# Layer 1's input projections by head pairs, as half tiles between the attention units

## Chip, cores and metric

The kernel runs on one core of one Trainium2 chip. The metric is the device time of one execution in microseconds (us); the number that counts is the median of the runs.

## What is computed

A two-layer transformer with two streams of 256 tokens each (latent and context, 1024 wide). Each layer has a mixer and then a hierarchical mixture of 32 experts. Layer 0's mixer is a window attention beside a latent attention; layer 1's, the one concerned here, is a differential attention with 8 heads:

```python
def _diff_mixer(h_lat, h_ctx, w_in, ..., subln, w_out, lambda_init, rope, ctx_out):
    q, k, v = _split(h @ w_in, DIFF_IN_WIDTHS)       # 1024 columns each, for both streams
    q: (b, n, 8, 2, 64)   k: (b, n, 8, 2, 64)   v: (b, n, 8, 128)
    q1_l, q2_l, k1_l, k2_l = _rope(...)              # latent stream only
    k1_all = concat([k1_l, k1_c]); k2_all, v_all likewise   # 512 keys
    a1 = _dense_attention(q1_l, k1_all, v_all, scale)
    a2 = _dense_attention(q2_l, k2_all, v_all, scale)
    o = _rmsnorm(a1 - lam * a2, subln, DIFF_EPS) * (1.0 - lambda_init)
    return o @ w_out                                 # the latent stream alone in the last layer
```

Behind it stand the residual, the norm, the router, the top two of 32 experts for 256 tokens, and a final norm.

## The kernel before

All in float32. A product that needs accuracy is made of three passes: each operand is split into a high part (float32r) and a low part, and `mm3` (line 397) multiplies high by high, high by low and low by high for each of 8 slices of the contraction. `split` (line 389) makes the high part on ScalarE (line 392), or on another engine given as `first` (line 394), and the low part by a subtraction on the engine given as `eng` (line 395).

**Loads.** Every weight comes as a tile of 128x2048 elements (1 MB) through one queue on SyncE, in the order in which `plan` lists it: the 12 tiles of layer 1's input weights (`dwin`, in the order `DWO`, with the tiles of an adaLN part between them as `ADO` says), four tiles of another adaLN part, the four tiles of the output weights (`wout1`), four more adaLN tiles, and then the experts of layer 1, six tiles each. The first four experts are fixed; the others depend on the router, and `limits` holds their loads until it has spoken. The tiles lie in a pool of 24 slots that they share with the data. `budget(n)` says that n slots are kept for data; `pump` (line 172) issues loads while the loaded tiles are below 24 less that (or less the data that stand now).

**Weight splits.** `Splits` (line 406): a `step` splits half a tile (128 columns of 256 for each of 8 slices), `get` hands out the split tile and, unless told otherwise, makes the next one at once, with the low part on VectorE.

**Layer 1's projections.** Tiles 0 to 3 of `DWO`'s numbers are queries, 4 to 7 keys, 8 to 11 values; each holds two heads. `DWO` gives the order 4, 5, 6, 8, 0, 7, 9, 1, 10, 2, 11, 3. The first key tile goes through `proj_step` into two banks `psA`; the eleven others through `k_tile`, `q_tile` and `v_tile` (lines 1665 to 1696), one after the other, each with two halves, before the first attention unit. A key half is one accumulation of 24 matmuls of 512 columns, a query half 24 of 256 (latent tokens only), a value half 48 of 256. Key and query halves get the rotary embedding in `rope_lat` (line 566: one product with the cosines in line 570, four with the sines in 573, an addition in 574, all on VectorE), then a split with the low part on GpSimd. A key half's context columns are copied by ScalarE (line 1661), a value half is copied by ScalarE (line 1694).

**Layer 1's attention.** A unit is a head and one of two query tiles of 128: 16 units. `run_units` (line 776) writes the order out by hand, and the program's order is each engine's order. In step i: scores and maximum of unit i+2; the hook of i (`early1`, line 1791); the values (`d_pv`) of unit i-1; an adaLN step, where the given function says so; the scaling (`d_scale`) of i+1; the transposes of i; the exponentials of i+2. A unit is, on TensorE, 6 score matmuls (line 1721), 4 transposes (1753) and 4 value matmuls (1765, shown as 8); on VectorE two maxima (1728), a small product (1729), a reciprocal, a small scaling (1744), the scaling and subtraction of the two maps (1746) and the output (1769); on ScalarE two exponentials (1736), a copy (1755) and a square (1768). `early1` also sets budgets, splits half tiles of the output weights on GpSimd alone (`Wo.step(GP, GP)`, at hooks 7, 9, 11 and 13) and starts the norm of the output at the end. Behind the last unit `d_turn` transposes the output, and `out_block` multiplies it with the output weights.

PSUM gives scores four banks (`psA`) and pieces, transposes and values three (`psB`).

Of the kernel before, what the change touches and what calls it, by code (L numbers as in the profile page):

```python
# [19 lines left out]
P = 128  # L20
# [32 lines left out]
DWO = (4, 5, 6, 8, 0, 7, 9, 1, 10, 2, 11, 3)  # L53
ADO = {0: (0, 1), 1: (2, 3, 4), 2: (5,), 3: (6,), 4: (7,)}
# [62 lines left out]
def model_kernel(ctx: ExitStack, tc: tile.TileContext, xin, small, cst, ada0, adaw, win, wuq, wukv, wout0, dwin,  # L117
# [24 lines left out]
    def free(n):  # L142
        st_["data"] -= n
# [422 lines left out]
    def rope_lat(ps, dst, p0, cosn, sinn):  # L566

        t = U((SEQ,))
        r = U((SEQ,))
# [1080 lines left out]
    h_lo(1, KC - 1, xb, *h13(KC - 1), True)  # L1650
    fill(2)
# [6 lines left out]

    def k_out(j, ps):
        dst = U()  # L1660
        ACT.copy(dst[:, SEQ:], ps[:, SEQ:])
        rope_lat(ps, dst, 0, "cosA", "sinA")
        split(*(x[j // 4].v[:, j % 4, :] for x in k1), dst, GP)

    def k_tile(j2):
        ws = W1.get()
        for j in range(2):
            ps = psB()
            s = slice(j * P, (j + 1) * P)
            mm3(ps, KC, lambda k: (ws[0][:, k, s], ws[1][:, k, s]), h13)  # L1670
            k_out(2 * j2 + j, ps)
        free(2)

    def q_tile(j2):
        ws = W1.get()
        for j in range(2):
            ps = psB()
            s = slice(j * P, (j + 1) * P)
            mm3(ps[:, 0:SEQ], KC, lambda k: (ws[0][:, k, s], ws[1][:, k, s]),
                lambda k: tuple(x[:, 0:SEQ] for x in h13(k)))  # L1680
            dst = U((SEQ,))
            rope_lat(ps, dst, 0, "cosA", "sinA")
            split(*(x.v[:, 2 * j2 + j, :] for x in q1), dst, GP)
        free(2)

    def v_tile(j):
        ws = W1.get()
        for t2 in range(2):
            ps = psB()
            for t in range(2):  # L1690
                ts_ = slice((2 * t2 + t) * P, (2 * t2 + t + 1) * P)
                mm3(ps[:, t * 256:(t + 1) * 256], KC, lambda k: tuple(x[:, ts_] for x in h13(k)),
                    lambda k: (ws[0][:, k, :], ws[1][:, k, :]))
            ACT.copy(v1[j // 2].v[:, 2 * t2:2 * t2 + 2, (j % 2) * 256:(j % 2 + 1) * 256],
                     ps.rearrange("p (t n) -> p t n", t=2))
        free(2)
# [11 lines left out]
    budget(18)  # L1708
    for j in DWO[1:]:
        (q_tile, k_tile, v_tile)[j // 4](j % 4)  # L1710
    free(4)
# [300 lines left out]
```

## Time and profile before

| | us |
|---|---|
| median of 3 runs | 1483.35 (1480.6 to 1484.48) |
| the profiled execution | 1484.73 |
| its span, first to last instruction | 1482.6 |
| TensorE busy | 1304.1 (88% of the span) |
| VectorE busy | 602.1 (41%) |
| ScalarE busy | 384.5 (26%) |
| GpSimd busy | 128.0 (9%) |

The profile is one execution on the chip. PE is TensorE's matmuls, PEld its weight loads, DVE VectorE, ACT ScalarE, POOL GpSimd, SPq the load queue of SyncE. A row of a timeline gives the start in us, the duration in us, engine, line, operation, output and inputs, and how many instructions it merges; in brackets stands the idle time in front of it and what ended that. Matmuls overlap in their records, so the distance from start to start is what one costs. PEclk is the granted clock of TensorE, 1.00 being 2.4 GHz.

### The profile page before, as it was taken

What the parts mean: (1) busy time and instruction counts of PE and PEld (TensorE: products, weight loads), DVE (VectorE), ACT (ScalarE), POOL (GpSimd) and SP (SyncE); (2) the same over time, 40 slices, a digit from 0 to 9 for tenths busy, and PEclk for the clock granted to TensorE, in tenths of its full rate; (3) what the DMA queues carried; (4) which work ended last, traced back from release to release, by engine and by line L of the source; (5) the groups of instructions that cost most, each with busy time, mean ns of one, the idle gap of its engine ahead of it and who ended that gap; (6) DMA issues with size and microseconds to landing.
All of it is one profiled execution on the core that took longest, in us unless ns stands there. A gap on an engine that the chain in (4) does not pass through costs nothing.

```text
span 1482.6 us, 21587 instructions
## 1 busy us (share of the span) xinstructions
PE 1304.1 (88%) x8341; PEld 724.3 (49%) x8341; DVE 602.1 (41%) x1476; ACT 384.5 (26%) x819; POOL 128.0 (9%) x110
## 2 busy tenths in 40 slices
PE   6996999989999999989878999888998787788856
PEld 4673667955445343525326897584442231323313
DVE  4488896453322322222227756944321110111102
ACT  4445655331111110101115333643110010101002
POOL 1134011220000000000013111301000000000000
PEclk9998999999999999999999999999999999998999
DMA  9634715279999999999999228357999999999995
GB/s 382 266 114 152 273 48 211 90 307 374 399 420 422 421 421 420 421 422 420 408 412 382 86 86 304 135 219 276 422 420 422 421 421 420 422 421 421 421 412 228
DMA packets 70075, 487.08 MB, mean 329 GB/s; under 512 B 7632, under 2 KB 7760, under 8 KB 13392
## 3 DMA queue, kind: packets, MB, share of 16 engines
q1 hardware_dynamic: 69968, 485.65, 80.7%
q8 instruction: 68, 1.11, 0.3%
q14 instruction: 39, 0.32, 0.1%
HBM read 484.57 MB, written 1.05 MB: 328 GB/s over the span
## 4 chain that ended last, share of the span: by engine, by line
DMA 25%; PE 16%; DVE 6%; ACT 2%; issue 1%; DVEq 0%; SPq 0%; ACTq 0%
DMA s<-in_ew_dram 25%; PE psA L1336 3%; PE psA L1368 3%; PE psB L403 2%; PE psB L404 2%; PE psB L402 2%; DVE t L1728 1%; DVE u L1746 1%; DVE s L395 1%; PE psA L402 1%; PE psA L403 1%; PE psA L404 1%; PE psB L1385 1%; DVE u L573 0%; DVE s L1378 0%
## 5 line engine op out<-in xcount | busy, mean ns | idle before, releaser
L1336 PE MATMUL psA<-s 128*32 128x512 f32 (+2 forms) x2336 | 418.3, 621 | 81.4 <-DMA s<-in_ew_dram 71.6
L1336 PEld LDWEIGHTS psA<-s 128*32 128x32 f32 (+2 forms) x2336 | 113.7, 122 | 362.7 <-issue 206.2
L1378 DVE SCALAR_TENSOR_TENSOR s<-psB,modT,s 128x256 f32<-128x256 f32 x296 | 120.4, 476 | 215.6 <-PE psB L1385 215.5
L1368 PE MATMUL psA<-s,u 128*32 128x512 f32 (+1 forms) x1168 | 185.9, 601 | 12.8 <-DMA s<-in_ew_dram 11.4
L1373 DVE SCALAR_TENSOR_TENSOR u<-psA,t,u 128x512 fp32r<-128x512 f32 x48 | 36.0, 751 | 233.0 <-ACT u L1372 233.0
L1368 PEld LDWEIGHTS psA<-s,u 128*32 128x32 f32 (+1 forms) x1168 | 53.6, 119 | 123.7 <-issue 95.4
L1510 DVE TENSOR_TENSOR u<-u,psA 128x512 f32<-128x512 f32 x24 | 16.5, 688 | 224.3 <-PE psA L1336 224.3
L1385 PE MATMUL psB<-u 128*128 128x512 f32 (+1 forms) x384 | 95.8, 369 | 13.1 <-DVE s L1378 4.6
L1362 ACT COPY u<-psB 128x512 f32<-128x512 f32 x24 | 14.1, 587 | 332.6 <-PE psB L1360 332.6
L402 PE MATMUL psB<-s 128*128 128x256 f32 (+1 forms) x296 | 96.0, 324 | 3.9 <-DVE s L895 3.9
L403 PE MATMUL psB<-s 128*128 128x256 f32 (+1 forms) x296 | 95.2, 322 | 0.4 <-DVE s L395 0.4
L404 PE MATMUL psB<-s 128*128 128x256 f32 (+1 forms) x296 | 95.1, 321 | 0.0
L1385 PEld LDWEIGHTS psB<-u 128*128 128x128 f32 x384 | 58.7, 188 | 72.1 <-issue 35.7
L1372 ACT ACTIVATE u<-psA,t 128x512 fp32r<-128x512 f32 x48 | 33.0, 688 | 177.2 <-PE psA L1368 171.6
L1507 ACT ACTIVATE u<-psA 128x512 f32<-128x512 f32 x24 | 14.4, 600 | 220.8 <-PE psA L1336 220.8
L1319 PE MATMUL psB<-s 128*128 128x256 f32 x544 | 68.0, 285 | 0.7 <-ACT u L1362 0.7
L395 DVE TENSOR_TENSOR s<-s 128x1024 fp32r<-128x1024 f32 (+3 forms) x56 | 51.6, 967 | 39.9 <-ACT s L392 39.8
L1319 PEld LDWEIGHTS psB<-s 128*128 128x128 f32 x544 | 65.9, 191 | 2.6 <-issue 1.6
L402 PEld LDWEIGHTS psB<-s 128*128 128x128 f32 x296 | 56.4, 190 | 13.8 <-DVE s L895 4.8
L402 PE MATMUL psA<-s 128*128 128x256 f32 (+1 forms) x208 | 62.6, 301 | 0.0
L403 PE MATMUL psA<-s 128*128 128x256 f32 (+1 forms) x208 | 60.5, 291 | 0.0
L404 PE MATMUL psA<-s 128*128 128x256 f32 (+1 forms) x208 | 60.4, 291 | 0.0
(349 smaller groups left out, 1736.6 us busy)
## 6 DMA issues: line engine op xcount, KB each, us to landing
s<-in_ew_dram SPq DMA_DIRECT2D x376, 1024.0 KB, 19.8
s<-in_adaw_dram SPq DMA_DIRECT2D x40, 1024.0 KB, 7.5
s<-in_dwin_dram SPq DMA_DIRECT2D x12, 1024.0 KB, 10.3
s<-in_ada_dram SPq DMA_DIRECT2D x8, 1024.0 KB, 19.8
s<-in_wout_dram SPq DMA_DIRECT2D x8, 1024.0 KB, 7.7
s<-in_ew_dram SPq DMA_DIRECT2D x16, 512.0 KB, 14.4
s<-in_win_dram SPq DMA_DIRECT2D x5, 1024.0 KB, 19.9
s<-in_xin_dram SPq DMA_DIRECT2D x2, 1024.0 KB, 8.6
```

Of the source, the lines that this page charges most:

```text
L395: eng.tensor_tensor(lo, src, hi.bitcast(F32), ALU.subtract)
L402: PE.matmul(ps, lh, rh, start=(k == 0), stop=False)
L403: PE.matmul(ps, lh, rl, start=False, stop=False)
L404: PE.matmul(ps, ll, rh, start=False, stop=(k == n - 1))
L1319: PE.matmul(ps[:, i * n:(i + 1) * n], src(t, cs_(c0 + i)), oh[:, t, 0:n], start=(t == 0 and a == 0), stop=(t == T_ - 1 and a == 1))
L1336: PE.matmul(ps[sl, :], xg(hf * 4 + k, sl), wt(m, hf)[:, k, :], start=(hf == 0 and k == 0), stop=(hf == 1 and k == 3))
L1368: PE.matmul(ps[sl, :], ht[:, k, sl], wt(2, hf)[:, k, :], start=(k == 0), stop=(k == 3))
L1372: ACT.activation(yh, ps, AF.Copy, scale=gsl)
L1373: DVE.scalar_tensor_tensor(out=yl, in0=ps, scalar=gsl, in1=yh.bitcast(F32), op0=ALU.mult, op1=ALU.subtract)
L1378: DVE.scalar_tensor_tensor(out=xc(c)[:, HALF[s]], in0=ps[:, HALF[s]], scalar=modT[:, l, 5, c, s:s + 1], in1=xc(c)[:, HALF[s]], op0=ALU.mul ...
L1385: PE.matmul(ps[:, 0:nt], ysp[a][:, cs_(q)], oht[:, 0:nt], start=(a == 0), stop=(a == 1))
L1510: TT(hm, sl, pm[1], ALU.mult)
```

## The change

The key, query and value tiles come in the order of head pairs: key 0, query 0, value 0, key 1, query 1 and so on (`DWO`), and the adaLN tiles that go with them move (`ADO`). `k_tile`, `q_tile` and `v_tile` become `k_piece`, `q_piece` and `v_piece`, which do one half each. `piece` takes the next half from a list, and behind it issues the split of half a tile of weights for the tile after it, with the low part on GpSimd (`W1.step(GP)`). The first four halves (query 0, value 0) stand ahead of the units, with the scores and exponentials of units 0 and 1 between them; the other 18 stand in the hooks of units 0 to 12, one or two each (`PIECES`). The hook runs behind the scores of unit i+2. The steps of the output weights move from hooks 7, 9, 11, 13 to 12, 13, 14, 15, the adaLN steps to hooks 2, 6, 10 and on, and the budgets change. Temporaries of the rotary embedding, the query halves and the squares move from the pool `u` to the context halves of the residual (`room`, eight in turn), which nothing reads any more.

```diff
--- before.py
+++ after.py
@@ -50,8 +50,10 @@
 
 ADL = 3
 
-DWO = (4, 5, 6, 8, 0, 7, 9, 1, 10, 2, 11, 3)
-ADO = {0: (0, 1), 1: (2, 3, 4), 2: (5,), 3: (6,), 4: (7,)}
+PIECES = {0: 1, 1: 2, 2: 1, 3: 1, 4: 2, 5: 2, 6: 1, 7: 1, 8: 2, 9: 2, 10: 1, 11: 1, 12: 1}
+
+DWO = (4, 0, 8, 5, 1, 9, 6, 2, 10, 7, 3, 11)
+ADO = {0: (0, 1), 1: (2, 3, 4), 5: (5,), 8: (6,), 11: (7,)}
 
 
 
@@ -563,10 +565,9 @@
     DVE.tensor_copy(UB, csv("U"))
 
 
-    def rope_lat(ps, dst, p0, cosn, sinn):
-
-        t = U((SEQ,))
-        r = U((SEQ,))
+    def rope_lat(ps, dst, p0, cosn, sinn, tr=None):
+
+        t, r = tr or (U((SEQ,)), U((SEQ,)))
         DVE.tensor_tensor(t[p0:P], ps[p0:P, 0:SEQ], csv(cosn)[p0:P], ALU.mult)
         for q in range(p0 // 32, 4):
             a, b = slice(32 * q, 32 * q + 32), slice(32 * (q ^ 1), 32 * (q ^ 1) + 32)
@@ -1648,6 +1649,7 @@
             W1.step()
         xb = xa
     h_lo(1, KC - 1, xb, *h13(KC - 1), True)
+    budget(19)
     fill(2)
     ps = psB()
     PE.matmul(ps[:, 0:2], onesM, lp, start=True, stop=True)
@@ -1656,44 +1658,57 @@
     DVE.tensor_scalar(nlam, lamt[:, 2:3], -LAMBDA_INIT, None, op0=ALU.add)
     k1 = [[S((4, NTOK), F32R) for _ in range(2)] for _ in range(2)]
 
+
+    rooms_ = [0]
+
+    def room():
+        rooms_[0] += 1
+        return xc(rooms_[0] % KC)[:, SEQ:]
+
     def k_out(j, ps):
         dst = U()
         ACT.copy(dst[:, SEQ:], ps[:, SEQ:])
-        rope_lat(ps, dst, 0, "cosA", "sinA")
+        rope_lat(ps, dst, 0, "cosA", "sinA", (room(), room()))
         split(*(x[j // 4].v[:, j % 4, :] for x in k1), dst, GP)
 
-    def k_tile(j2):
-        ws = W1.get()
-        for j in range(2):
-            ps = psB()
-            s = slice(j * P, (j + 1) * P)
-            mm3(ps, KC, lambda k: (ws[0][:, k, s], ws[1][:, k, s]), h13)
-            k_out(2 * j2 + j, ps)
-        free(2)
-
-    def q_tile(j2):
-        ws = W1.get()
-        for j in range(2):
-            ps = psB()
-            s = slice(j * P, (j + 1) * P)
-            mm3(ps[:, 0:SEQ], KC, lambda k: (ws[0][:, k, s], ws[1][:, k, s]),
-                lambda k: tuple(x[:, 0:SEQ] for x in h13(k)))
-            dst = U((SEQ,))
-            rope_lat(ps, dst, 0, "cosA", "sinA")
-            split(*(x.v[:, 2 * j2 + j, :] for x in q1), dst, GP)
-        free(2)
-
-    def v_tile(j):
-        ws = W1.get()
-        for t2 in range(2):
-            ps = psB()
-            for t in range(2):
-                ts_ = slice((2 * t2 + t) * P, (2 * t2 + t + 1) * P)
-                mm3(ps[:, t * 256:(t + 1) * 256], KC, lambda k: tuple(x[:, ts_] for x in h13(k)),
-                    lambda k: (ws[0][:, k, :], ws[1][:, k, :]))
-            ACT.copy(v1[j // 2].v[:, 2 * t2:2 * t2 + 2, (j % 2) * 256:(j % 2 + 1) * 256],
-                     ps.rearrange("p (t n) -> p t n", t=2))
-        free(2)
+    def k_piece(j2, j, ws):
+        ps = psB()
+        s = slice(j * P, (j + 1) * P)
+        mm3(ps, KC, lambda k: (ws[0][:, k, s], ws[1][:, k, s]), h13)
+        k_out(2 * j2 + j, ps)
+
+    def q_piece(j2, j, ws):
+        ps = psB()
+        s = slice(j * P, (j + 1) * P)
+        mm3(ps[:, 0:SEQ], KC, lambda k: (ws[0][:, k, s], ws[1][:, k, s]),
+            lambda k: tuple(x[:, 0:SEQ] for x in h13(k)))
+        dst = room()
+        rope_lat(ps, dst, 0, "cosA", "sinA", (room(), room()))
+        split(*(x.v[:, 2 * j2 + j, :] for x in q1), dst, GP)
+
+    def v_piece(j, t2, ws):
+        ps = psB()
+        for t in range(2):
+            ts_ = slice((2 * t2 + t) * P, (2 * t2 + t + 1) * P)
+            mm3(ps[:, t * 256:(t + 1) * 256], KC, lambda k: tuple(x[:, ts_] for x in h13(k)),
+                lambda k: (ws[0][:, k, :], ws[1][:, k, :]))
+        ACT.copy(v1[j // 2].v[:, 2 * t2:2 * t2 + 2, (j % 2) * 256:(j % 2 + 1) * 256],
+                 ps.rearrange("p (t n) -> p t n", t=2))
+
+
+    pieces = [(j, n) for j in DWO[1:] for n in range(2)]
+    cur = []
+
+    def piece(n=1):
+        for _ in range(n):
+            j, i = pieces.pop(0)
+            if i == 0:
+                cur.append(W1.get(False))
+            (q_piece, k_piece, v_piece)[j // 4](j % 4, i, cur[0])
+            W1.step(GP)
+            if i:
+                cur.pop()
+                free(2)
 
     wl = [W1.get(False)]
     pss = [psA() for _ in range(2)]
@@ -1705,12 +1720,7 @@
     free(2)
     q1 = [S((KC, SEQ), F32R) for _ in range(2)]
     v1 = [S((4, 512)), S((4, 512))]
-    budget(18)
-    for j in DWO[1:]:
-        (q_tile, k_tile, v_tile)[j // 4](j % 4)
-    free(4)
     oD = S((16, P))
-    budget(11)
 
     def d_scores(u):
         h, qt = u
@@ -1764,7 +1774,7 @@
         for b in range(4):
             PE.matmul(ps[:, 0:P], PT[:, b * P:(b + 1) * P], v1[h // 4].v[:, b, (h % 4) * P:(h % 4 + 1) * P],
                       start=(b == 0), stop=(b == 3))
-        sq = U((P,))
+        sq = room()[:, 0:P]
         ACT.activation(sq, ps[:, 0:P], AF.Square, scale=rec, accum_out=ssD[:, 0, 2 * h + qt:2 * h + qt + 1])
         DVE.tensor_scalar(oD.v[:, 2 * h + qt, :], ps[:, 0:P], rec, None, op0=ALU.mult)
 
@@ -1789,12 +1799,14 @@
         DVE.scalar_tensor_tensor(out=lo, in0=ps, scalar=sl1, in1=hi.bitcast(F32), op0=ALU.mult, op1=ALU.subtract)
 
     def early1(i):
-        if i in {2: 13, 10: 14}:
-            budget({2: 13, 10: 14}[i])
+        piece(PIECES.get(i, 0))
         if i == 9:
             free(3)
-            budget({2: 13, 10: 14}[10])
-        if i in (7, 9, 11, 13):
+            budget(16)
+        if i == 12:
+            free(4)
+            budget(14)
+        if i in (12, 13, 14, 15):
             Wo.step(GP, GP)
         if i == 14:
 
@@ -1808,8 +1820,12 @@
             d_norm(2)
             d_turn(1)
 
-    run_units([(h, qt) for h in range(8) for qt in range(2)], d_scores, d_max, d_exp, d_scale, d_transpose, d_pv,
-              lambda i: i in (1, 2, 3, 14, 15), early1, 3)
+    units = [(h, qt) for h in range(8) for qt in range(2)]
+    piece(2)
+    ex1 = {i: d_exp(units[i], *d_max(units[i], d_scores(units[i]))) for i in range(2)}
+    piece(2)
+    run_units(units, d_scores, d_max, d_exp, d_scale, d_transpose, d_pv,
+              lambda i: i in (2, 6, 10, 11, 12, 13, 14, 15), early1, ex=ex1)
     d_rstd(12, 16)
     d_norm(3)
     d_turn(2)
```

## Rows read from the trace of the kernel before

**Rows 1.** Busy time by stretches: length, PE, PEld, DVE, ACT, POOL, clock, DMA, GB/s.
```profile
805.20:907.60 102.40, 102.05 (x721) 96.07 (x719) 63.72 (x112) 33.00 (x51) 14.80 (x14) 1.00 0.36 126
907.60:976.70 69.10, 56.70 (x372) 38.28 (x371) 60.90 (x132) 43.77 (x122) 15.90 (x10) 0.90 0.62 241
...
1086.30:1455.60 369.30, 296.12 (x1662) 103.84 (x1662) 54.67 (x137) 33.64 (x59) 1.90 (x1) 0.95 1.01 420
```

**Rows 2.** Timeline of the load queue (SPq), 911 us to 1030 us.
```profile
911.24 99.84 SPq L170 DMA_DIRECT2D s<-in_ew_dram  x19
...
1028.25 0.80 SPq L170 DMA_DIRECT2D s<-in_ew_dram  x2
```

**Rows 3.** Timeline of PE: first matmuls of the projection halves, and the last.
```profile
805.21 0.39 PE L402 MATMUL psB<-s 128*128 128x512 f32 x1
...
826.97 0.28 PE L402 MATMUL psB<-s 128*128 128x256 f32 x1
...
907.47 0.28 PE L404 MATMUL psB<-s 128*128 128x256 f32 x1
```

**Rows 4.** Timeline of PE, one unit: scores, values, adaLN, transposes, next scores.
```profile
924.50 0.97 PE L1721 MATMUL psA<-s 64*128 64x512 f32 x6
925.39 1.16 PE L1765 MATMUL psB<-s,u 128*128 128x128 f32 x8
926.48 1.07 PE L324 MATMUL psC<-s,scS 128*32 128x512 f32 x8
927.48 0.65 PE L1753 MATMUL psB<-identR,u 128*128 128x128 f32 x4
928.07 0.97 PE L1721 MATMUL psA<-s 64*128 64x512 f32 x6
```

**Rows 5.** Timeline of DVE: the first product and the addition of one rope.
```profile
809.96 0.42 DVE L570 TENSOR_TENSOR u<-psA,u 128x256 f32<-128x256 f32 x1 [1.00 <-ACT u L1661]
...
812.15 0.43 DVE L574 TENSOR_TENSOR u<-u 128x256 f32<-128x256 f32 x1
```

**Rows 6.** Groups by shape, 805.2 to 907.6 us: xcount | busy us, mean ns.
```profile
L395 DVE TENSOR_TENSOR s<-s 128x1024 fp32r<-128x1024 f32 x22 | 27.0, 1266 | 25.8 <-ACT s L392 25.8
...
L392 ACT CAST s<-s 128x1024 fp32r<-128x1024 f32 x20 | 20.0, 1048 | 0.0
...
L392 ACT CAST s<-u 128x256 fp32r<-128x256 f32 x7 | 2.8, 406 | 24.1 <-DVE u L574 24.1
```

**Rows 7.** Timeline of POOL: low parts of key, query and weight half.
```profile
813.37 1.30 POOL L395 TENSOR_TENSOR s<-u,s 128x512 fp32r<-128x512 f32 x1 [2.35 <-ACT s L392]
...
846.38 0.74 POOL L395 TENSOR_TENSOR s<-u,s 128x256 fp32r<-128x256 f32 x1 [10.40 <-ACT s L392]
...
927.72 2.38 POOL L395 TENSOR_TENSOR s<-s 128x1024 fp32r<-128x1024 f32 x1 [2.56 <-PE psC L324]
```

**Rows 8.** Timeline of DVE: the scaling of three units.
```profile
927.92 2.72 DVE L1746 SCALAR_TENSOR_TENSOR u<-u,t 128x512 f32<-128x512 f32 x1
...
944.78 0.75 DVE L1746 SCALAR_TENSOR_TENSOR u<-u,t 128x512 f32<-128x512 f32 x1
...
947.54 0.75 DVE L1746 SCALAR_TENSOR_TENSOR u<-u,t 128x512 f32<-128x512 f32 x1
```

**Rows 9.** Timeline of PE: three waits, start of the output projection.
```profile
938.10 1.12 PE L1753 MATMUL psB<-identR,u 128*128 128x128 f32 x4 [4.77 <-DVE u L1746]
...
968.59 0.66 PE L1753 MATMUL psB<-identR,u 128*128 128x128 f32 x4 [2.26 <-DVE u L1746]
...
976.07 0.63 PE L1786 MATMUL psB<-identR,s 128*128 128x128 f32 x4 [1.47 <-DVE s L1781]
976.45 0.36 PE L402 MATMUL psA<-s 128*128 128x256 f32 x1
```

**Rows 10.** Busy time by stretches, columns as in rows 1.
```profile
935.00:940.00 5.00, 1.90 (x8) 1.48 (x10) 4.93 (x5) 1.48 (x5) 4.84 (x4) 0.56 0.31 131
940.00:945.00 5.00, 4.86 (x28) 3.44 (x27) 4.82 (x12) 3.12 (x10) 1.38 (x1) 0.76 0.50 165
```

## Prediction

> **What bounds the kernel now.** I read the busy time by stretches first, from the end of the span backwards, then the load queue, then the timelines of the stage that changes. From 1086 us to 1456 us the load of expert weights is what TensorE waits for: the DMA share is 1.01 and 420 GB/s pass, about 2.5 us for a tile of 1 MB [rows 1]. So the end of the kernel is the time at which that stream gets going, plus a fixed volume. The stream can't go ahead of the router of layer 1: only the 24 tiles of the four fixed experts may be asked for before it, and the slots of SBUF run out at 19 of them; between 1011 us and 1028 us no load is issued at all, until the first expert matmuls free slots [rows 2]. Whatever moves the end of layer 1's mixer moves that restart by the same amount.
>
> The mixer has two stages. From 805.2 us (the end of the first key tile) to 907.6 us TensorE projects: 102.0 of 102.4 us busy at clock 1.00, VectorE 63.7. From 907.6 us to 976.5 us it does the sixteen attention units, the clock is 0.90, and VectorE has 60.9 of 69.1 us [rows 1]. The change can only win what TensorE loses in the second stage, so I count its work at full clock.
>
> - Projection halves, by the starts of their first matmuls: four key halves from 805.21 to 826.97, so 5.44 us each; the matmuls of 256 columns follow at 0.12 us, so a query half (24 of them) takes 2.88 us and a value half (48) 5.76 us [rows 3]. The 22 pieces that the change moves: 6 x 5.44 + 8 x 2.88 + 8 x 5.76 = 101.7 us.
> - One unit: scores 0.89, values 1.09, transposes 0.59, from start to start; an adaLN step 1.00 [rows 4]. Sixteen units 41.1 us; seven steps and two closings (0.6 each) 8.2 us; four turns of the output at 0.6, 2.4 us.
>
> Together 153.4 us. From 805.2 us that would end at 958.6 us; the output projection really starts at 976.45 us [rows 9]. The difference, 17.9 us, is all that a perfect interleave could win.
>
> **What the change moves, and what new waits cost.** It takes no matmul away. It puts TensorE's pieces between units, so that VectorE's 2.76 us per unit (the steady distance of two scalings [rows 8]) no longer sets the pace. For that it makes TensorE depend on fresh results within a few us, which the old order never did: there the scores began with data tens of us old. I walked through the new order with the old durations.
>
> *Durations off TensorE.* A rope runs from 809.96 to 812.58, 2.62 us, and for a key half it starts behind ScalarE's copy of the other half of the bank (it sat 1.00 us idle for it) [rows 5]. The high part of a query half is a ScalarE cast of 0.41 us, that of a weight half 1.05 us. The low part of a weight half was VectorE's at 1.27 us, 22 of them, 27.0 us, all under a busy TensorE, so taking them from VectorE gains nothing by itself [rows 6]. It becomes GpSimd's at 2.38 us; a low part of a key half takes 1.30 us there, of a query half 0.74 us [rows 7]. GpSimd works in order, so the low part of a query stands behind the weight half issued before it, and the next weight half behind the query.
>
> *Opening.* Both ropes of the first key tile end at 812.58 us as now. TensorE does Q0a and Q0b from 805.2 to 811.0 us and then wants the scores of unit 0. Q0a's rope can only start at 812.6 and ends at 815.2; its high part is there at 815.65. Wait: 4.65 us. Scores of two units end at 817.7. V0a then needs all 256 columns of its weights' low part (its second matmul reads them). GpSimd does Q0a's low part to 816.4, the first half of V0's weights to 819.0, Q0b's low part, the second half to about 823.0 (822.1 if nothing is held). Wait: 5.3 us, at least 4.4. Opening 10.0 us, at least 9.1.
>
> *Each later pair of heads.* The hook of units 1, 5 and 9 issues a key half and a query half; the next scores need that query half. Behind it TensorE has the values and transposes, 1.7 us. Until the low part is there: GpSimd gets the key's low part 3.7 us after the key half ends (copy, rope, cast), has it done at 5.0, the weight half at 7.35, the query's low part at 8.1 us; the query half ended at 2.88, so 5.2 us later. Four of the six score matmuls can go with the high part, 0.6 us. Wait: 5.2 - 0.6 - 1.7 = 2.9 us; if GpSimd were free it would be 1.5 us. The second wait is the value half's. The second half of its weights is cast and subtracted behind the second query half: rope 2.6, cast 0.4, cast of the weights 1.05, GpSimd 2.38: 6.4 us after that query half. TensorE has values, an adaLN step, transposes, scores and one matmul in between, 3.7 us. Wait: 2.7 us. So 5.6 us a pair, at least 4.2.
>
> *VectorE held by GpSimd.* A scaling of 128x512 that takes 0.75 us took 2.72 us when a GpSimd subtraction ran from 927.72 to 930.10; it ended 0.5 us behind that [rows 7, 8]. It reads two operands from SBUF. So does the last step of a rope, the addition in line 574, and no row shows that one held by a long subtraction: its price lies between 0 and 2.4 us each time it meets one. In the walk it meets one in the query rope of each pair (the weight half runs from 5.0 to 7.35, the addition is due at 5.2), of which 0.7 us reach TensorE after the order of GpSimd is counted. I take 0.7, nearer to the scaling's row than to nothing: 6.3 us a pair, three pairs 18.9 us.
>
> The Trainium skill states for this (SBUF — State Buffer, section SBUF: two separate sides) that a VectorE instruction with two SBUF inputs and a GpSimd instruction that reads SBUF exclude each other for the whole instruction, whoever comes first. The trace agrees for the scaling (2.72 against 0.75 us); for the addition no run here shows it. With the rule the addition is held and a pair waits 6.3 us; without it 5.6 us, and the sum would be 2.1 us lower. The rule speaks against the change, which gives GpSimd 22 more subtractions.
>
> *Closing.* Before, TensorE sat idle 2.26 us and 1.47 us in the chain from the last scaling to the output projection [rows 9]. That chain stays: 3.7 us.
>
> *Clock.* After the idle 4.77 us that ended at 938.10 [rows 9] the granted clock was 0.56 and 0.76 in the next two stretches of 5 us [rows 10]: 3.4 us at the lower level, 1.7 us of work lost. The opening has two idles of that size, 3.4 us. The six idles of some 3 us in the pairs may cost 1.7 us each too, or nothing: 0 to 10.2 us; I take nothing, since they are shorter.
>
> *Output weights.* The four steps of Wo, a cast and a subtraction on GpSimd each, stood in the middle of the attention; they belong to that 4.77 us idle and the low clock after it, 6.5 us. Now they stand behind GpSimd's last projection work, which ends about when V3a starts. If they run under V3a and V3b they cost nothing; if their slots come free only after V3b they hold VectorE in the last three units, where no piece covers it. 0 to 6.5 us; I take 0.
>
> *Loads.* The budget holds loads to five slots until unit 9, so the output weights, the last adaLN part and the expert tiles come later. From unit 9 to the end of the mixer there are about 50 us, twenty tiles at 2.5 us, and about 18 are needed to stand where the old kernel stood; the idle from 1011 us to 1028 us covers what is late. If it does not, each tile costs 2.5 us. The temporaries that move into dead halves of the residual cost nothing: they are the same instructions on the same shapes.
>
> **The sum.** 10.0 + 18.9 + 3.7 + 3.4 = 36.0 us of waiting and low clock where there were 17.9 us: 18.1 us longer. The profiled execution took 1484.73 us (span 1482.6 and 2.1 around it), the median of the runs is 1483.35 us; I add to the median: 1501 us.
>
> **The rivals.**
> - *The waits in the pairs vanish (faster).* If the ropes, casts and subtractions of a query half reach TensorE within the 1.7 us and 3.7 us of other work, only opening and closing are left: 9.1 + 3.7 = 12.8 against 17.9 us, 5.1 us shorter, 1478 us. It decides at 1.7 us of waiting a pair. For it: VectorE and GpSimd are each busy less than TensorE in the new stage. Against it: the rope alone is 2.62 us, and GpSimd's order is fixed. Chance 0.13.
> - *The waits are near that point (no change).* One of a pair's two waits hides and the other shrinks, so 1.7 to 3 us a pair: 1480 to 1487 us. Chance 0.07.
> - *The later router is partly absorbed.* 19 of the 24 fixed tiles are issued before it [rows 2]; were five more slots free by then, 12.5 us of the stream would be gone: 1489 us. Against it: the budgets at that place are unchanged. Chance 0.10.
> - *The costs left out come in full.* Low clock in the pairs 10.2 us and Wo 6.5 us: 1518 us. For it: the gaps come every 10 to 20 us. Chance 0.15.
> - That the loads come too late for the experts would look like the last one and is held in it.
>
> My forecast has 0.55. All but the first two cases are slower by over 0.3% (4.4 us, about what a measurement of this kernel can tell from no change): slower 0.80, same 0.07, faster 0.13. The least of the forecast's own terms, 9.1 + 3 x 4.2 + 3.7 = 25.4, gives 1491 us. The range goes from 1487, below that, to 1518.
>
> **What would show it.** In the trace after: PE idle of 4 to 5 us before the first scores and before the first value half; before the scores of units 4, 8 and 12 idle of about 3 us ended by a GpSimd subtraction; before V1a, V2a and V3a idle of about 2.7 us ended by one too; the additions of the query ropes longer than 0.43 us; the output projection starting near 994 us; the expert stream as long as before. If TensorE runs through these places, the first rival is right and my walk has a latency wrong. If the output projection starts late and the end does not follow, the loads are what I misread.

## The result

| | before | changed |
|---|---|---|
| median of the runs, us | 1481.97 (1480.48 to 1484.48) | 1520.94 (1515.97 to 1521.93) |
| profiled execution, us | 1484.73 | 1521.14 |
| its span | 1482.6 | 1519.4 |
| end of the first key tile | 805.0 | 803.1 |
| first matmul of the output projection | 976.45 | 1012.34 |
| from there to the end of the span | 506.2 | 507.1 |

The ratio is 1.0254, with an interval of 1.0226 to 1.0283: 39 us slower. The forecast was 1501 us, with a range up to 1518 us. The direction was right, the size half of what came.

Busy time of the changed kernel by stretches (length, PE, PEld, DVE, ACT, POOL, granted clock, DMA share, GB/s): the whole stage from the first key tile to the output projection, what follows up to the experts, and the eight stretches inside the stage in which the clock is at its lower level.

```profile
803.05:1012.34 209.29, 170.78 (x1090) 144.98 (x1089) 123.77 (x224) 75.59 (x172) 77.70 (x44) 0.88 0.37 138
1012.34:1053.00 40.66, 36.05 (x313) 33.15 (x311) 18.96 (x41) 14.95 (x29) 9.50 (x10) 1.00 0.67 265
811.20:824.90 13.70, 7.01 (x29) 5.50 (x30) 10.90 (x21) 5.89 (x13) 7.43 (x5) 0.50 0.19 61
855.60:862.40 6.80, 5.91 (x26) 5.12 (x27) 4.50 (x8) 3.54 (x9) 3.23 (x3) 0.50 0.00 0
869.20:872.60 3.40, 2.97 (x14) 2.97 (x15) 2.51 (x5) 0.14 (x2) 0.37 (x1) 0.50 0.02 5
906.80:913.60 6.80, 5.64 (x25) 4.85 (x26) 4.83 (x8) 3.54 (x9) 3.50 (x3) 0.50 0.00 0
920.40:923.80 3.40, 2.82 (x13) 2.82 (x14) 2.66 (x5) 0.28 (x2) 0.53 (x1) 0.50 0.11 45
958.00:964.80 6.80, 5.63 (x25) 4.84 (x26) 4.84 (x8) 3.53 (x9) 3.51 (x3) 0.50 0.45 159
971.60:975.00 3.40, 2.82 (x13) 2.82 (x14) 2.66 (x5) 0.78 (x4) 0.53 (x1) 0.50 0.94 381
1002.40:1009.20 6.80, 5.77 (x26) 5.52 (x27) 3.67 (x9) 2.11 (x5) 0.00 (x0) 0.50 1.01 424
```

Before, the two halves of this stage lasted 171.5 us, with the clock at 1.00 and 0.90 [rows 1]. Now it is one stage of 209.3 us at a mean clock of 0.88. All that the kernel lost is here: the part behind it takes 0.9 us more. In the eight short stretches the clock is at its lower level, 0.50 (1.2 GHz), through and through: 51.1 us, in 38.6 of which TensorE is busy. In the kernel before there are three such stretches with 13.6 us, 11.1 of them busy. Each of the eight begins inside one of TensorE's waits; the next view shows those of the opening, of two pairs and of the closing.

Timeline of PE in the changed kernel: the longest idle times of the opening, of the first two pairs of heads and of the closing (in brackets, with what ended them), and the start of the output projection:

```profile
813.92 2.93 PE L1731 MATMUL psA<-s 64*128 64x512 f32 x12 [4.73 <-ACT s L394]
818.98 0.58 PE L404 MATMUL psB<-s 128*128 128x256 f32 x1 [2.13 <-ACT s L394]
821.40 0.58 PE L405 MATMUL psB<-s 128*128 128x256 f32 x1 [1.84 <-POOL s L397]
...
856.50 1.65 PE L1731 MATMUL psA<-s 64*128 64x512 f32 x6 [3.40 <-ACT s L394]
...
867.21 0.38 PE L404 MATMUL psB<-s 128*128 128x256 f32 x1 [0.73 <-ACT s L394]
...
869.63 0.58 PE L405 MATMUL psB<-s 128*128 128x256 f32 x1 [2.04 <-POOL s L397]
...
907.96 1.65 PE L1731 MATMUL psA<-s 64*128 64x512 f32 x6 [4.76 <-ACT s L394]
...
918.55 0.38 PE L404 MATMUL psB<-s 128*128 128x256 f32 x1 [0.73 <-ACT s L394]
...
920.98 0.58 PE L405 MATMUL psB<-s 128*128 128x256 f32 x1 [2.04 <-POOL s L397]
...
1003.43 1.09 PE L1796 MATMUL psB<-identR,s 128*128 128x128 f32 x4 [3.90 <-DVE s L1791]
...
1012.34 0.36 PE L404 MATMUL psA<-s 128*128 128x256 f32 x1
```

L1731 are scores, L404 and L405 here the first and second matmul of a value half. The third pair repeats the second (4.70, 0.73 and 2.04 us); the six other idle times are 0.5 to 1.5 us each. The sum of all idle in the stage is 38.5 us; it was 12.6 us.

How the first wait of the second pair of heads comes about, seen from VectorE (timeline of the changed kernel; the additions that close a key rope and a query rope):

```profile
902.41 0.42 DVE L575 TENSOR_TENSOR u<-s 128x256 f32<-128x256 f32 x1
...
905.07 2.40 DVE L575 TENSOR_TENSOR s<-s 128x256 f32<-128x256 f32 x1
```

and from GpSimd (key half, weight half, query half):

```profile
903.62 1.27 POOL L397 TENSOR_TENSOR s<-u,s 128x512 fp32r<-128x512 f32 x1 [5.51 <-ACT s L394]
904.85 2.34 POOL L397 TENSOR_TENSOR s<-s 128x1024 fp32r<-128x1024 f32 x1
907.99 0.73 POOL L397 TENSOR_TENSOR s<-s 128x256 fp32r<-128x256 f32 x1 [0.80 <-ACT s L394]
```

and from ScalarE (the casts of the query half and of the next weight half):

```profile
907.51 1.35 ACT L394 CAST s<-s 128x256 fp32r<-128x256 f32 x2 [3.01 <-DVE s L575]
```

The key's addition takes 0.42 us, the query's 2.40: the weight half on GpSimd holds it from 905.07 to 907.2. The cast that waits for it starts at 907.51, the scores begin at 907.96 with the high part, and the query's low part follows on GpSimd at 907.99. It is the same hold as that of the scaling before [rows 8], now on an addition.

### The profile page after: what moved, and what is told of

It is laid out like the page before. It is cut to its first block, busy times and chain, and to the rows that moved or that the text cites. A ratio compares the mean times of both kernels' runs of the same rounds, so it can differ in the third digit from the quotient of the medians.

```text
span 1519.4 us, 21585 instructions
## 1 busy us (share of the span) xinstructions
PE 1321.8 (87%) x8341; PEld 734.4 (48%) x8341; DVE 601.1 (40%) x1456; ACT 383.1 (25%) x819; POOL 175.0 (12%) x130
## 4 chain that ended last, share of the span: by engine, by line
DMA 24%; PE 17%; DVE 6%; ACT 2%; issue 1%; POOL 1%; DVEq 0%; SPq 0%; POOLq 0%; ACTq 0%
DMA s<-in_ew_dram 24%; PE psA L1337 4%; PE psA L1369 2%; PE psB L405 2%; PE psB L404 2%; PE psB L406 2%; POOL s L397 1%; DVE s L574 1%; DVE s L575 1%; ACT s L394 1%; PE psA L1731 1%; PE psB L1320 1%; PE psA L404 1%; PE psA L405 1%; PE psB L1775 1%
## 5 line engine op out<-in xcount | busy, mean ns | idle before, releaser
L1337 PE MATMUL psA<-s 128*32 128x512 f32 (+2 forms) x2336 | 425.4, 637 | 75.7 <-DMA s<-in_ew_dram 66.9
L404 PE MATMUL psB<-s 128*128 128x256 f32 (+1 forms) x296 | 102.8, 347 | 9.4 <-ACT s L394 4.3
L405 PE MATMUL psB<-s 128*128 128x256 f32 (+1 forms) x296 | 100.8, 340 | 8.0 <-POOL s L397 8.0
L397 POOL TENSOR_TENSOR s<-s 128x1024 fp32r<-128x1024 f32 (+1 forms) x40 | 82.0, 2052 | 199.6 <-ACT s L394 135.5
L1511 DVE TENSOR_TENSOR u<-u,psA 128x512 f32<-128x512 f32 x24 | 16.5, 688 | 223.0 <-PE psA L1337 223.0
L406 PE MATMUL psB<-s 128*128 128x256 f32 (+1 forms) x296 | 99.9, 337 | 0.5 <-POOL s L397 0.5
L404 PEld LDWEIGHTS psB<-s 128*128 128x128 f32 x296 | 61.5, 208 | 25.3 <-issue 8.7
L405 PEld LDWEIGHTS psB<-s 128*128 128x128 f32 x296 | 61.8, 209 | 12.5 <-POOL s L397 8.8
L1320 PEld LDWEIGHTS psB<-s 128*128 128x128 f32 x544 | 65.9, 191 | 2.6 <-issue 1.6
L394 ACT CAST s<-s 128x1024 fp32r<-128x1024 f32 (+3 forms) x71 | 53.8, 799 | 40.7 <-DVE s L575 32.2
L406 PEld LDWEIGHTS psB<-s 128*128 128x128 f32 x296 | 61.6, 208 | 5.0 <-POOL s L397 0.7
## 6 DMA issues: line engine op xcount, KB each, us to landing
s<-in_ew_dram SPq DMA_DIRECT2D x376, 1024.0 KB, 19.8
s<-in_dwin_dram SPq DMA_DIRECT2D x12, 1024.0 KB, 11.9
s<-in_ew_dram SPq DMA_DIRECT2D x16, 512.0 KB, 14.5
```

Of the source, the lines that this page charges most:

```text
L394: ACT.copy(hi, src)
L397: eng.tensor_tensor(lo, src, hi.bitcast(F32), ALU.subtract)
L404: PE.matmul(ps, lh, rh, start=(k == 0), stop=False)
L405: PE.matmul(ps, lh, rl, start=False, stop=False)
L406: PE.matmul(ps, ll, rh, start=False, stop=(k == n - 1))
L1320: PE.matmul(ps[:, i * n:(i + 1) * n], src(t, cs_(c0 + i)), oh[:, t, 0:n], start=(t == 0 and a == 0), stop=(t == T_ - 1 and a == 1))
```

## The experiments

Each starts from the changed kernel unless it says otherwise. Stage is the time from the end of the first key tile to the output projection in the profiled execution; idle is the sum of TensorE's idle in it; the rest is stage less idle less the 153.4 us of work at full clock.

| kernel | time, us | stage | idle | rest |
|---|---|---|---|---|
| before | 1482 to 1483 | 171.5 | 12.6 | 5.5 |
| changed | 1520.9 | 209.3 | 38.5 | 17.4 |
| e1_split_ahead | 1501.3 | 190.2 | 27.7 | 9.1 |
| e2_query_unit_ahead | 1521.9 | 211.0 | 41.1 | 16.5 |
| e3_four_pieces_first | 1529.2 | 217.9 | 44.7 | 19.8 |
| e4_keep_busy | 1512.6 | 202.1 | 20.8 | |
| e5_low_part_on_vector | 1519.0 | 206.8 | 38.9 | 14.5 |
| e6_ahead_vector | 1507.9 | 194.7 | 32.0 | 9.3 |
| e7_all_waits | 1495.7 | 182.9 | 22.4 | 7.1 |
| e8_all_waits_vector | 1504.8 | 192.1 | 27.5 | 11.2 |
| e9_sum_from_psum | 1500.1 | 188.2 | 25.0 | 9.8 |
| e10_waits_and_psum | 1495.9 | 183.4 | 22.6 | 7.4 |
| e11_before_wo | 1477.3 | 164.7 | 11.1 | 0.2 |
| e12_after_wo | 1520.5 | 209.2 | 38.9 | 16.9 |

The rest of e4 is left out, since it has more matmuls. Three things stand in this table before any single run is read. The stage's length carries the time of the kernel: from 6.8 us less (e11) to 46 us more (e3) than before, the time differs by as much within 3 us. And the rest grows with the idle: with 22 to 28 us of idle it is 7 to 11 us, with 38 to 45 us it is 14 to 20 us. And e11, the one run whose clock is 1.00 in the whole stage, has a rest of 0.2 us, so the 153.4 us of work hold.

**Weights split ahead of the piece.**

```diff
-            (q_piece, k_piece, v_piece)[j // 4](j % 4, i, cur[0])
             W1.step(GP)
+            (q_piece, k_piece, v_piece)[j // 4](j % 4, i, cur[0])
```

> Starts from the changed kernel (1520.9 us). One edit: the half tile of weights for the next tile is split ahead of the piece, not behind it, so that its cast and its GpSimd subtraction no longer stand behind the rope and split of the query half. Theory (the order of GpSimd and ScalarE makes TensorE wait): the waits of the value halves (2.0 + 0.7 us, three pairs, and 4.0 us in the opening) go, and the waits of the scores fall from 3.4 to 4.8 us to some 1.5 to 2.5 us, because the low part of the query half has only its rope in front of it; idle 38.5 us falls by 17 to 20 us, and some of the low clock behind the waits goes with it: 1491 to 1504 us. Rival (the rope's own time makes the waits): only the value halves gain, 8 us, 1511 to 1514 us. Rival (GpSimd's hold on VectorE makes them): as many holds as before, so no gain, 1518 to 1523 us.

1501.3 us (1.0129 of before, 1.0106 to 1.0153): 19.6 us faster than the change, the largest step of all. The waits of the value halves are gone, as the theory of the order wants. The waits of the scores are not down to 1.5 to 2.5 us, and that of the opening grew from 4.73 to 6.74 us. Timeline of PE:

```profile
849.13 1.60 PE L1731 MATMUL psA<-s 64*128 64x512 f32 x6 [4.05 <-ACT s L394]
...
894.96 1.65 PE L1731 MATMUL psA<-s 64*128 64x512 f32 x6 [4.39 <-ACT s L394]
```

and of POOL (weight half, then the query's low part):

```profile
846.02 2.34 POOL L397 TENSOR_TENSOR s<-s 128x1024 fp32r<-128x1024 f32 x1
849.15 0.73 POOL L397 TENSOR_TENSOR s<-s 128x256 fp32r<-128x256 f32 x1 [0.80 <-ACT s L394]
```

The cast of the weight half still stands behind the key half's cast on ScalarE, so its subtraction lands on the query's addition (2.41 us long, from 846.23) as before. Order is the cause of the value waits; for the score waits this run leaves order and hold together.

**The query half a unit earlier.** `PIECES` becomes 3, 1, 1, 1 for each pair in place of 1, 2, 1, 1, 2 and so on.

```diff
-PIECES = {0: 1, 1: 2, 2: 1, 3: 1, 4: 2, 5: 2, 6: 1, 7: 1, 8: 2, 9: 2, 10: 1, 11: 1, 12: 1}
+PIECES = {0: 3, 1: 1, 2: 1, 3: 1, 4: 3, 5: 1, 6: 1, 7: 1, 8: 3, 9: 1, 10: 1, 11: 1}
```

> Starts from the changed kernel. One edit: the first query half of a pair comes one unit earlier (three pieces in the hooks of units 0, 4 and 8, one in the others), so a whole piece stands between it and the scores that need it. Theory: the three waits of the scores (3.4, 4.8 and 4.7 us) go and those of the value halves (2.0 + 0.7 us a pair) stay; idle falls by 11 to 13 us and low clock by some 5 us: 1502 to 1510 us. Rival (the waits only move to the next piece, since GpSimd has the same work in the same order): 1517 to 1523 us.

1521.9 us, no gain: the theory's number was wrong and the rival's right. The scores of the pairs no longer wait; the value half does, twice as long (5.5 in place of 2.8 us). Timeline of PE:

```profile
867.52 0.58 PE L404 MATMUL psB<-s 128*128 128x256 f32 x1 [3.61 <-ACT s L394]
...
869.95 0.58 PE L405 MATMUL psB<-s 128*128 128x256 f32 x1 [1.84 <-POOL s L397]
```

Three pieces in one hook bunch the ropes and splits, and the value half behind them takes the wait over. The additions of the three query ropes that moved took 0.43, 0.51 and 0.58 us, so the hold is nearly gone here, and the idle is 41.1 us all the same. Room for one consumer is taken from another as long as the chain ahead of both has the same length.

**Four pieces before the first scores.** `piece(4)` stands ahead of `ex1`, and the second `piece(2)` goes.

> Starts from the changed kernel. One edit: all four pieces of the opening come before the scores of units 0 and 1. Theory (what TensorE waits for in the opening is the low part of the second half of the value weights, behind two query halves on GpSimd, and the scores in between are covered by that): the wait moves from the scores to the value half, which begins at the same time as now; nothing is won and the scores come behind it: 1520 to 1524 us. Rival (the place of the scores is the cause): 4.7 us and their low clock go, 1513 to 1517 us.

1529.2 us, 8 us slower, 5 us beyond the theory's interval. The wait moves to the value half, as the theory said:

```profile
820.51 0.58 PE L404 MATMUL psB<-s 128*128 128x256 f32 x1 [9.76 <-ACT s L394]
```

and behind it the scores of unit 2 wait 3.3 us for the exponentials that empty their banks, which the theory did not have.

**Matmuls in the waits.**

```diff
     def v_piece(j, t2, ws):
+        if t2 == 0:
+            idle(8)
...
+    def idle(n):
+        ps = psB()
+        for _ in range(n):
+            PE.matmul(ps, identR, h13(0)[0], start=True, stop=True)
...
     def d_scores(u):
         h, qt = u
+        if u == (0, 0):
+            idle(20)
+        if u in ((2, 0), (4, 0), (6, 0)):
+            idle(12)
```

> Starts from the changed kernel. Matmuls that nothing reads are added where TensorE waits: 20 before the scores of unit 0, 12 before those of units 4, 8 and 12, 8 before the first half of each value tile, 0.23 us each; they fit into the waits at full clock. Theory (17 us of the 55.6 us that the stage loses are the lower level of the clock, which follows the waits): the clock stays near 1.00 in the stage and 8 to 14 us come back, 1507 to 1513 us, with the waits as long as before. Rival (the clock falls for another reason than TensorE's waiting): no change, or up to 3 us slower, 1520 to 1524 us.

1512.6 us (1.0204, 1.0181 to 1.0226): with more work on TensorE the kernel is 8.3 us faster. The stage, same columns as above:

```profile
800.83:1002.95 202.12, 181.19 (x1179) 150.58 (x1177) 123.87 (x224) 75.59 (x172) 78.03 (x44) 0.97 0.39 143
```

The clock is 0.97 in place of 0.88 and the stage 7.2 us shorter. TensorE is busy at the lower level for 11.4 us in place of 38.6. So the lower level of the clock that comes with the waits is a cost of its own, of at least this size: the 88 added matmuls take some 20 us themselves (88 times 0.23), and the idle falls by 17.7 us only. They do not fill all waits (1.0 to 1.9 us stay ahead of the three groups of 12, for their bank), and one of these groups ran at the lower level itself.

**The low part on VectorE**, behind the piece (`W1.step(DVE)`) and then also ahead of it.

> Starts from the changed kernel (1520.9 us). One edit: the low part of the weight halves goes back from GpSimd to VectorE, in the same place behind the piece. Theory (order): VectorE then holds no rope addition behind GpSimd, but the subtraction stands in VectorE's own queue, between the ropes of the key and the query half, behind ScalarE's cast, so the score waits stay at 4 to 5 us; the value waits fall by 1.1 us a pair, and the opening's by about 2 us: 1513 to 1519 us. Rival (GpSimd's hold on the rope addition, 2 us each, is the greater part of the waits): 8 to 10 us of idle and their low clock go, 1502 to 1509 us.

> Both edits: weights split ahead of the piece and their low part on VectorE. The first alone gave 1501.3 us; its three score waits are 4.1 to 4.4 us and in each the addition of the query rope is held 2.0 us by GpSimd's weight half. Theory (order): the weight half's subtraction takes the same place in VectorE's queue, since ScalarE casts it behind the key half; the score waits stay: 1498 to 1505 us. Rival (hold): three times 2 us and some low clock go, 1490 to 1496 us.

1519.0 and 1507.9 us. Taking all weight halves off GpSimd, and with them every hold on a rope (all additions take 0.42 or 0.43 us), gains nothing that the intervals show (1.0198 to 1.0269 of before, against 1.0226 to 1.0283), and where they are split ahead it is 6.5 us slower by the medians (1.0146 to 1.0202 against 1.0106 to 1.0153). Timeline of PE in the first of the two:

```profile
907.42 1.65 PE L1731 MATMUL psA<-s 64*128 64x512 f32 x6 [5.24 <-ACT s L394]
...
919.50 0.38 PE L405 MATMUL psB<-s 128*128 128x256 f32 x1 [0.88 <-DVE s L397]
```

The score wait is 5.2 us and so longer than with the hold (4.76), the second part of the value wait 0.9 in place of 2.0 us. VectorE works in order too, and its subtraction now stands between the two ropes. So the rival's gain does not come by this way; but the hold is exchanged here for 1.3 us of work on VectorE, and what the hold alone is worth is seen in e9. e6 came out slower than the theory had it.

**All waits at once.** Split ahead; value tile 0 ahead of query tile 0 in `DWO`; `piece(5)` ahead of the first scores and no `piece(2)` behind them; `PIECES` 2, 1, 1, 1 and then 3, 1, 1, 1 twice. The second with `W1.step(DVE)`.

> Everything that the waits rest on is moved: weights split ahead of the piece, the first query half of a pair one unit earlier, the first value tile ahead of the first query tile, and the scores of units 0 and 1 behind the first key half of pair 1. GpSimd keeps the low parts. Theory (what the change loses is its waits and the low clock behind them): idle falls from 38.5 us to the closing's 7 us and 2 to 4 us more, the low clock from 17 us to 3 to 6 us; the stage then loses 12 to 17 us against 17.9 us in the kernel before: 1475 to 1483 us. Rival (holds between GpSimd and VectorE and the three PSUM banks make new waits as the old ones go): 1488 to 1500 us.

> As e7_all_waits, with the low part of the weight halves on VectorE. Theory (order; with room in front of every consumer it doesn't matter which engine subtracts): within 4 us of e7_all_waits. Rival (hold): 5 us or more faster than it.

1495.7 us (1.0096, 1.0067 to 1.0125) and 1504.8 us. The idle falls by 16 us and the rest by 10 us, but not as far as expected, and the kernel stays slower than before; the rival's range holds. Timeline of PE in the first:

```profile
834.97 2.31 PE L1731 MATMUL psA<-s 64*128 64x512 f32 x6 [4.41 <-ACT u L1746]
...
900.16 0.36 PE L404 MATMUL psB<-s 128*128 128x256 f32 x1 [1.94 <-DVE s L574]
```

The scores of unit 2 wait for the exponentials that empty their banks (4.41 us), and the first value half of a pair waits 1.4 to 1.9 us until the rope has read the bank of the query half ahead of it. Those are the rival's new waits, on PSUM banks. On VectorE it is 9 us worse, which neither theory had.

**The addition without the hold**, on top of e1.

```diff
-        DVE.tensor_tensor(t[p0:P], ps[p0:P, 0:SEQ], csv(cosn)[p0:P], ALU.mult)
+        if tr:
+            t = ps[:, 0:SEQ]
+        else:
+            DVE.tensor_tensor(t[p0:P], ps[p0:P, 0:SEQ], csv(cosn)[p0:P], ALU.mult)
...
+        if tr:
+            DVE.tensor_tensor(t, t, csv(cosn), ALU.mult)
         DVE.tensor_tensor(dst[p0:P, 0:SEQ], t[p0:P], r[p0:P], ALU.add)
```

> e1_split_ahead (1501.3 us) with one more edit: the rope's product with the cosines stays in PSUM, so that its last addition reads one operand from PSUM and one from SBUF instead of two from SBUF. The number of VectorE instructions and their order stay. Theory (GpSimd's weight half holds the addition of the query rope for 2 us, and that alone is taken away here): the additions take 0.4 to 0.5 us again, the three score waits fall from 4.1 to 4.4 us to 2.1 to 2.5 us and the opening's from 6.7 to 4.7 us; 8 us of idle and some low clock go: 1489 to 1495 us. Rival (the addition is held whatever it reads, or the query's low part then waits for the weight half on GpSimd all the same): 1499 to 1504 us.

1500.1 us against 1501.3, no difference that the intervals show (1.0107 to 1.0138 and 1.0106 to 1.0153); that is the rival's range, and the theory's 8 us did not come. Timeline of DVE, the addition of the query rope, while GpSimd runs weight and query half from 850.06 to 853.1:

```profile
850.31 0.42 DVE L580 TENSOR_TENSOR s<-psB,s 128x256 f32<-128x256 f32 x1
```

0.42 us: one operand in PSUM, and it is not held. Timeline of PE:

```profile
851.23 0.73 PE L1736 MATMUL psA<-s 64*128 64x512 f32 x4 [2.13 <-ACT s L394]
853.16 0.50 PE L1736 MATMUL psA<-s 64*128 64x512 f32 x2 [1.20 <-POOL s L397]
```

The high part of the scores now waits 2.1 us, and the low part another 1.2 us, for GpSimd, which does the weight half first. So the hold is real, and order stands right behind it: 4.1 to 4.4 us became 3.3. The stage is 2.0 us shorter.

**Waits and addition together.** e7 with this addition, and `piece(4)`, `ex1`, `piece(1)`.

> e7_all_waits (1495.7 us) with the rope's addition from PSUM as in e9_sum_from_psum, and the scores of units 0 and 1 ahead of the first key half of pair 1 again (in e7 those of unit 2 wait 4.4 us for their banks). Theory: the opening's 4.4 us falls to 1.5 to 2 us, the holds go; the bank of a query half is read 0.4 us longer, so the 1.9 us waits of the value halves stay: 1486 to 1492 us, that is still not faster than the kernel before, since the closing's 7 us and some low clock stay. Rival (without waits the interleave wins what it was meant to win): 1470 to 1480 us.

1495.9 us, as e7. The opening's 4.4 us is gone, and the first value half of a pair waits 3.4 to 3.8 us for the bank in place of 1.4 to 1.9, since the rope now works in it. The forecast was too low; that it would not beat the kernel before held.

**The output weights off GpSimd**, `Wo.step()` in place of `Wo.step(GP, GP)`, in the kernel before and in the changed one.

> The kernel before (1483 us), with the four early steps of the output weights off GpSimd: the high part on ScalarE, the low part on VectorE. It measures the term of the output weights by itself. Theory (their two GpSimd instructions hold VectorE and cost TensorE 4.8 us idle and 1.7 us of low clock): 6.5 us go and 4 x 1.2 us of VectorE's time come in, where VectorE sets the pace: 1480 to 1484 us. Rival (what follows the waits, the low clock, is worth more than the idle): 1474 to 1479 us.

> The changed kernel (1520.9 us) with the four early steps of the output weights off GpSimd, as e11_before_wo does it to the kernel before. It measures the closing: in the changed kernel these steps run at 988 to 1002 us, behind the last value half, and the last two scalings of VectorE are held 2.1 us each by them, with idle of 3.9 us and low clock of some 3.5 us behind it. Theory (that is the steps' cost in the closing): 4 to 8 us go, 1513 to 1517 us. Rival (the closing waits for its own chain, and VectorE and ScalarE, which now split the weights between the last units, take what GpSimd gave): 1518 to 1523 us.

In the kernel before it gives 1477.3 us, 0.9963 of it (0.9949 to 0.9977): faster than both kernels, and in the rival's range. Its second half of the stage, columns as above:

```profile
907.50:969.50 62.00, 51.33 (x369) 33.82 (x368) 56.03 (x136) 46.84 (x126) 1.47 (x2) 1.00 0.69 267
```

62 us at clock 1.00 in place of 69.1 at 0.90 [rows 1]; the wait of 4.77 us [rows 9] and the low clock behind it are gone. In the changed kernel it gives nothing (1520.5 us). There the closing waits 5.27 us in place of 3.90; timeline of PE:

```profile
1003.63 1.11 PE L1796 MATMUL psB<-identR,s 128*128 128x128 f32 x4 [5.27 <-DVE s L1791]
```

and of DVE (the last scaling, the low part of a weight half, the norm that the wait is for):

```profile
1000.56 0.75 DVE L1756 SCALAR_TENSOR_TENSOR u<-u,t 128x512 f32<-128x512 f32 x1
1001.75 1.22 DVE L397 TENSOR_TENSOR s<-s 128x1024 fp32r<-128x1024 f32 x1 [0.44 <-ACT s L394]
1002.89 1.28 DVE L1791 TENSOR_TENSOR s<-s,ssD 128x512 f32<-128x512 f32 x2
```

The scalings are no longer held (0.75 us; 2.86 and 2.88 in the changed kernel), but VectorE now waits for ScalarE's cast and splits the weights right ahead of the norm, as the rival had it. The closing's idle is not owed to GpSimd's hold alone; no run leaves both out.

## Why the prediction was wrong

The direction was right, and TensorE waits in each of the places that the forecast named. The waits, forecast against measured: before the first scores 4.65 and 4.73 us; before the first value half 5.3 and 4.0; before units 4, 8 and 12 3.6 and 3.4, 4.8, 4.7; before the value halves 2.7 and 2.8. One sign did not come: the waits before units 4, 8 and 12 end with ScalarE's cast of the query's high part and not with a GpSimd subtraction. The walk had the order of GpSimd as the greater part of these waits and the held addition as 0.7 us; in the trace the held addition and the cast behind it set their end, and the order of GpSimd stands right behind (e9).

The addition of the query rope was held: 2.40 against 0.42 us in the changed kernel, and 0.42 with one input in PSUM. This agrees with the rule of the Trainium skill (SBUF — State Buffer, section SBUF: two separate sides) for two SBUF inputs. By the rule the forecast was 6.3 us a pair, without it 5.6; measured were 6.7, 8.1 and 8.1. What the hold is worth to the whole is less than its length: e9 takes it away and the time stays. GpSimd got 20 more subtractions and not 22 (44 instructions in the stage, 24 before [rows 1]), on which no term rests.

The size failed in one step above all, the clock. The forecast took low clock for the opening's two waits, 3.4 us, and set the six waits of the pairs at nothing "since they are shorter". The trace shows the clock at 0.50 with the wait of 3.40 us as with those of 4.7, and with the value waits of 0.73 and 2.04 us too. The kernel before spoke against the step already. Its wait of 2.26 us ended at 968.59 us [rows 9], and right behind it the clock is at its lower level (columns as above):

```profile
969.70:973.10 3.40, 3.40 (x19) 3.40 (x18) 1.68 (x7) 1.32 (x4) 0.00 (x0) 0.50 0.79 335
```

The price of one wait was misread too: 0.56 and 0.76 in two stretches of 5 us [rows 10] are 6.8 us at the lower level, not 3.4; TensorE was busy in 4.3 of them, which is some 2.1 us of work lost, not 1.7.

Half of TensorE's busy time in the eight stretches gives an estimate of what the lower level cost in the changed kernel: 3.5 us in the opening, 12.9 us in the pairs, 2.9 us in the closing, 19.3 us together. The forecast had 3.4, 0 and 0; that the opening agrees, with a price that was misread, is luck. The terms, in us:

| term | forecast | measured |
|---|---|---|
| opening | 10.0 | 8.7 |
| pairs | 18.9 | 22.8 |
| closing | 3.7 | 7.0 |
| low clock and the rest | 3.4 | 17.4 |
| sum | 36.0 | 55.9 |

14.0 of the 19.9 us that were missing are the last line, and the estimate of 19.3 us covers all of its 17.4: by it the line is the lower level of the clock alone. That the waits bring it about is shown by e4: with the waits filled, 8.3 us come back in spite of the added work. The pairs' 3.9 us come from the second and third pair. There the query rope starts later, behind a key rope that ends later on VectorE, and its addition is held longer. Timeline of DVE, the first product and the addition of the query rope in the first pair, and the first product in the second:

```profile
851.87 0.42 DVE L571 TENSOR_TENSOR s<-psB,u 128x256 f32<-128x256 f32 x1 [0.51 <-PE psB L406]
...
854.06 1.94 DVE L575 TENSOR_TENSOR s<-s 128x256 f32<-128x256 f32 x1
...
902.87 0.42 DVE L571 TENSOR_TENSOR s<-psB,u 128x256 f32<-128x256 f32 x1
```

The query half's last matmul starts at 851.48 and 901.59 us, so the rope starts 0.39 and 1.28 us behind it, and the additions take 1.94 and 2.40 us: together the 1.36 us by which the score wait grows. An idle of 0.6 us ahead of the key half, ended by a rope's product, comes on top. The closing's 3.3 us is what the forecast left open under the output weights, 0 to 6.5, and took as 0; e12 shows that it is not to be had by moving them off GpSimd.

Two sums of the prediction leave the low clock of the opening out although its waits stay in: the first rival's 12.8 us and the least of 25.4 us. With its 3.4 us they are 16.2 and 28.8 us, which gives 1482 and 1494 us in place of 1478 and 1491. The order of the rivals was wrong too. The case of "the costs left out come in full", with chance 0.15 and 1518 us, is nearest to what happened. The range ended at its sum, 52.7 us of waiting and low clock, where 55.9 came. That this is so near is partly luck, since its parts are off both ways: its low clock was 13.6 us (3.4 and 10.2) against 17.4 measured, its closing 10.2 against 7.0, its pairs 18.9 against 22.8, its opening 10.0 against 8.7.

The other steps held. 17.9 us was the most to be won, and no variant of the change won any of it: e7 and e10, with the idle down from 38.5 to 22.4 and 22.6 us, have 29.5 and 30.0 us of idle and rest in the stage, against 18.1 before. The stream of expert weights did follow the mixer one to one, 506.2 against 507.1 us; the loads that come later cost 0.9 us at most. The term of the output weights in the kernel before, 6.5 us, came out in its sum: in e11 the stage is 6.8 us shorter and the kernel 5 us faster. Its parts did not: forecast were 4.8 us of idle and 1.7 us of low clock, measured are 1.5 us of idle (12.6 to 11.1) and 5.3 us of the rest (5.5 to 0.2), so here too the clock was put too low.

## What to carry to other kernels

When work of a busy engine is put between units of a chain, look first at the helpers' queues: the preparation of the next piece belongs ahead of the piece, not behind its results (19.6 us here, for two lines exchanged). Count the length of each new wait of TensorE and then the clock behind it: here 25.9 us of added idle came with 11.9 us of further loss, and 8.3 us came back when matmuls filled a part of the waits. A wait that is moved and not shortened comes back at the next consumer, or at the PSUM banks.

## What was not expected of the chip

TensorE's granted clock fell to its lower level with waits as short as 0.73 and 2.04 us, one shortly behind the other, and in the kernel before behind one of 2.26 us; in e11 it stayed at 1.00 behind one of 2.06 us, and no run here shows what makes the difference. Adding matmuls that nobody reads made the kernel 8.3 us faster. A VectorE addition whose inputs both lie in SBUF is held until a GpSimd subtraction ends (2.40 us), and not at all (0.42 us) when one lies in PSUM. The hold also stretches the smallest instructions: a VectorE product of two columns took 2.18 us beside a weight half, and 0.17 us without one. Timeline of POOL and DVE in the changed kernel:

```profile
846.43 2.39 POOL L397 TENSOR_TENSOR s<-s 128x1024 fp32r<-128x1024 f32 x1
846.66 2.18 DVE L1739 TENSOR_SCALAR t<-t 128x2 f32<-128x2 f32 x1
...
900.14 0.17 DVE L1739 TENSOR_SCALAR t<-t 128x2 f32<-128x2 f32 x1
```
